# The low parts of four more projection weight blocks are formed on POOL instead of VectorE

## The chip, the cores and the metric

The kernel runs on one core of a Trainium2 chip. The metric is the device time of one execution in microseconds (us); the kernel before took 667.89 us in the median of three runs (666.8 to 670.55).

## The reference, cut to what matters

One layer of a backbone over 512 latent tokens and 256 context tokens of width 1024, float32:

```python
h_lat = modulate(rms_norm(x, norm1_w[layer]), sh1, sc1)
h_ctx = modulate(rms_norm(ctx, norm1_w[layer]), csh1, csc1)
p_lat = h_lat @ w_in[layer]
p_ctx = h_ctx @ w_in[layer]
y_ssd_lat, y_ssd_ctx = ssd_group(...)     # bidirectional Mamba-2 scan
y_ml_lat, y_ml_ctx = mlstm_group(...)     # bidirectional mLSTM
y_lat = concatenate([y_ssd_lat, from_col_major(y_ml_lat, rows)], axis=-1)
x = x + g1 * (y_lat @ w_out[layer])
x = x + g2 * hmoe(modulate(rms_norm(x, norm2_w[layer]), sh2, sc2), ...)
return rms_norm(x, final_norm_w)
```

The columns of `w_in` give z, x, B, C and the step sizes of the Mamba group and the inputs of the mLSTM group. The change lies in the product with `w_in`.

## The kernel before, in words

The product with `w_in` is made in float32r, with three matmuls for one: each operand is split into a high part H, which is the value cast to float32r, and a low part L, which is the value minus H. `mm3` (L255 to L260) adds H times H, H times L and L times H for each of eight slices of 128 rows. Each 256 columns of `w_in` come as two weight blocks of 128 x 1024 (512 KB): block `w3_0` holds slices 0 to 3 of column group 3, `w3_1` slices 4 to 7. A block passes four steps in `unit_w` (L221 to L231): SyncE's queue loads it (`raw_w`, L215, two buffers), ScalarE casts the high part (L224), and then VectorE or POOL subtracts to form the low part. A letter of the string `LENG` (L68), counted over the calls, says which: D is VectorE (L230), P is POOL (L228). High and low parts have three buffers each. The calls run in the order w2 (x), w3 (x), w0 and w1 (z), w4 (B), w5 (C) and on, two letters for each.

```python
        S.copy(wH, raw)
        e_ = LENG[nun[0]]
        nun[0] += 1
        if e_ == "P":
            wsub[0] = G.tensor_tensor(wL, raw, wH, ALU.subtract)
        else:
            V.tensor_sub(wL, raw, wH)
```

The order of the instructions on each engine is not the order of the source. A scheduler sets it when the program is built, by its own cost model; on the chip each engine then runs its list in that order, and semaphores make it wait for its inputs. So a letter of `LENG` can also move other instructions.

Around the change the program does these things side by side:

- `sx_block(1)` multiplies with w3: `sx1_0`, `sx1_1` and `sx1_c` (context). The `z` loop (L622 to L632) multiplies with w0 (`z0`, `z1`) and w1 (`z2`, `z3`). `sx_block(2)` and `sx_block(3)` multiply with w4 (B) and w5 (C). `conv` (L471 to L478) applies a convolution to each result: ScalarE at L473, four VectorE operations at L126, ScalarE's silu.
- `mod_late` (L589 to L606) streams blocks `wl` of 1 MB of the modulation weights (L191, three buffers) and multiplies them at L597 into `modl`; ScalarE copies the sum (`mrl`, L603) and two transposes follow (L606). `wl3_6` is the last block of `mod_late(3)`; `wl4_0` is the first of `mod_late(4)`.
- The gate chain of both groups is on VectorE: a polynomial `gp`, `tsp`, `ga`, then two scans `gF` (L505, L506), which read `ga` and the mask `rmask`, four scans `gm` (L507 to L510), the sums `gG`, `tsp`, `gW` (L520, L521, L118), and `gd`. The mask is three memsets on POOL (L498 to L500); `tsp` is cleared on POOL too (L492). PE's matmul `pgl` (L537) reads `gd`; transposes `gt` (L552, L557) follow, and from them `cw` and `cxw`, which the Mamba stage needs.
- The Mamba stage (L646 to L735) and the mLSTM stage follow, then the experts (MoE) from some 420 us on, where PE multiplies with expert weights that stream in.

Of the kernel before, what the change touches and what calls it, by code (L numbers as in the profile page):

```python
# [64 lines left out]
LASTC = ((0, 512), (512, 256), (768, 256))  # L65
FNS = (1, 3)
RG = [(0, 2), (2, 3), (3, 4)]
LENG = "PPDPDDDPDPDDPPDDDDDDDDPDPPPDPPPP"  # L68
OOB = float(1 << 20)
R2 = 44  # L70
C4N = 9
# [13 lines left out]
def body(tc, a, out, dbg=None):  # L85
# [135 lines left out]
    def unit_w(name, src, sc=None, to=None, raw=None):  # L221
        raw = raw or raw_w(name, src, sc=sc)
        wH, wL = to or (wst.tile([128, 1024], F32R, name=name + q, tag="w" + q, bufs=3)[:, :] for q in "HL")
# [3 lines that stand above are left out]
# [1396 lines left out]
```

## Time and profile before

| | |
|---|---|
| runs | 670.55, 666.8, 667.89 us; median 667.89 |
| profiled execution | 666.7 us, its span 665.0 us |
| PE busy | 606.8 us (91% of the span) |
| VectorE (DVE) busy | 406.8 us (61%) |
| ScalarE (ACT) busy | 271.4 us (41%) |
| POOL busy | 140.8 us (21%) |
| mean granted clock of TensorE | 0.972 of full speed |

PE is the busiest engine, so the places that count are those where PE stands idle or runs at a low clock, and what ends its idle time there. A share of the whole span doesn't tell of them; the table of stretches and the timelines do. The profiled execution lies 1.2 us under the median.

### The profile page before, as it was taken

The page shows a single profiled execution, that of the slowest core. Times are in us where ns is not written, and L with a number is a line of the kernel's source. Part 1 is how long each engine was busy: PE and PEld are TensorE (multiplying, and loading weights), DVE is VectorE, ACT ScalarE, POOL GpSimd, SP SyncE. Part 2 cuts the span into 40 slices and gives each one's busy share as a digit, 9 for nine tenths or more (in the row PEclk, how much of TensorE's full clock was granted, in tenths as well). Part 3 has the DMA queues.
Part 4 walks back from the last instruction along what each step waited for, and adds up shares of the span by engine and source line. Part 5 has one row for each costly group of instructions (what it writes and reads, how often), then busy time and mean ns, then how long its engine had stood idle before and what let it go on. Part 6 is the DMA issues. An engine that isn't in the chain of part 4 may idle for free. (4 is left out here: it accounts for less than half of the span.)

```text
span 665.0 us, 11431 instructions
## 1 busy us (share of the span) xinstructions
PE 606.8 (91%) x4315; PEld 414.7 (62%) x4315; DVE 406.8 (61%) x870; ACT 271.4 (41%) x580; POOL 140.8 (21%) x141
## 2 busy tenths in 40 slices
PE   4898997998899999999998995889999999998992
PEld 3574764787777888999998885524433334433341
DVE  2758996358756656545989765435555555555465
ACT  5435623428625694464254343122222222222325
POOL 2202000203776430023748010000000000000003
PEclk9999997999999999899999999799999999999996
DMA  8885787214435751137033798599999999999913
GB/s 342 313 292 192 299 293 281 91 38 134 162 108 184 283 178 34 31 122 268 14 118 125 289 416 372 209 422 422 426 423 425 391 382 398 410 424 412 411 66 126
DMA packets 35163, 171.64 MB, mean 258 GB/s; under 512 B 4435, under 2 KB 6051, under 8 KB 22052
## 3 DMA queue, kind: packets, MB, share of 16 engines
q1 hardware_dynamic: 31568, 162.68, 63.2%
q0 software_dynamic: 2448, 6.30, 2.4%
q10 hardware_dynamic: 1092, 1.93, 0.8%
q8 instruction: 34, 0.56, 0.3%
q14 instruction: 21, 0.17, 0.1%
HBM read 169.21 MB, written 4.30 MB: 261 GB/s over the span
## 5 line engine op out<-in xcount | busy, mean ns | idle before, releaser
L1308 PE MATMUL gu<-we,xT 128*32 128x512 f32 (+1 forms) x736 | 98.7, 603 | 0.6 <-DVE xT L123 0.6
L118 DVE TENSOR_TENSOR x1t<-x1t,pa 128x512 f32<-128x512 f32 (+1 forms) x108 | 66.2, 663 | 50.2 <-PE pa L1308 50.0
L1308 PEld LDWEIGHTS gu<-we,xT 128*32 128x32 f32 (+1 forms) x736 | 26.1, 114 | 50.3 <-issue 42.7
L1220 POOL DMA_INDIRECT xg<-xnd,tabi x13 | 13.2, 1015 | 192.9 <-PE xt L1308 166.9
L1308 PE MATMUL yy<-we,hTm 128*32 128x512 f32 (+2 forms) x384 | 49.1, 578 | 1.9 <-ACT hTm L1346 1.0
L1336 ACT ACTIVATE hid<-gu 128x256 f32<-128x256 f32 x13 | 5.0, 385 | 107.2 <-PE gu L1308 107.2
L1308 PE MATMUL pa<-yH,oh 128*128 128x512 f32 (+1 forms) x108 | 47.7, 445 | 0.5 <-DVE x1t L118 0.5
L1308 PE MATMUL pa<-yL,oh 128*128 128x512 f32 (+1 forms) x108 | 41.8, 391 | 0.8 <-DVE yL L1362 0.8
L1308 PEld LDWEIGHTS pa<-yH,oh 128*128 128x128 f32 x108 | 20.2, 188 | 31.5 <-issue 12.6
L1321 ACT ACTIVATE xT<-xt,mv,mv 128x128 f32<-128x128 f32 x78 | 29.8, 455 | 19.1 <-DVE xT L123 19.1
L228 POOL TENSOR_TENSOR w_1L<-w,w_1H 128x1024 fp32r<-128x1024 f32 x5 | 12.2, 2437 | 101.1 <-ACT w_1H L224 101.1
L1308 PEld LDWEIGHTS yy<-we,hTm 128*32 128x32 f32 (+1 forms) x384 | 14.8, 113 | 27.9 <-issue 21.6
L126 DVE SCALAR_TENSOR_TENSOR cv<-sx,pc,cv 128x510 f32<-128x510 f32 (+1 forms) x32 | 23.7, 741 | 11.2 <-ACT cv L473 10.9
L118 DVE TENSOR_TENSOR yf<-yy,g2b 128x512 f32<-128x512 f32 (+1 forms) x27 | 18.1, 672 | 18.9 <-PE yy L1308 17.5
L1361 ACT CAST yH<-yf 128x512 fp32r<-128x512 f32 (+1 forms) x27 | 16.2, 601 | 31.1 <-DVE yf L118 31.1
L1362 DVE TENSOR_TENSOR yL<-yf,yH 128x512 fp32r<-128x512 f32 (+1 forms) x27 | 19.0, 704 | 13.0 <-ACT yH L1361 12.2
L1308 PEld LDWEIGHTS pa<-yL,oh 128*128 128x128 f32 x108 | 20.4, 190 | 5.6 <-issue 1.4
L228 POOL TENSOR_TENSOR w_0L<-w,w_0H 128x1024 fp32r<-128x1024 f32 x3 | 7.6, 2547 | 74.7 <-ACT w_0H L224 74.7
L711 ACT ACTIVATE sg<-sg,cu 128x128 f32<-128x128 f32 x64 | 19.6, 388 | 9.4 <-POOL sg L648 9.4
L597 PE MATMUL modl<-wl,cs 128*32 128x256 f32 x256 | 18.1, 382 | 2.7 <-DMA wl<-in_w_mod_dram 2.7
L282 PE MATMUL mod<-wm,cs 128*32 128x256 f32 x128 | 12.2, 443 | 7.9 <-DMA wm<-in_wm_dram 7.9
L1308 PEld LDWEIGHTS xt<-ident,xg 128*128 128x128 f32 x104 | 12.0, 144 | 11.7 <-issue 10.9
(539 smaller groups left out, 1676.0 us busy)
## 6 DMA issues: line engine op xcount, KB each, us to landing
we<-in_wex_dram SPq DMA_DIRECT2D x94, 1024.0 KB, 8.1
wl<-in_w_mod_dram SPq DMA_DIRECT2D x16, 1024.0 KB, 5.7
w<-in_win_dram SPq DMA_DIRECT2D x24, 512.0 KB, 4.1
wm<-in_wm_dram SPq DMA_DIRECT2D x8, 1024.0 KB, 5.4
sg<-rowS SPq DMA_DIRECT2D x8, 512.0 KB
sw<-rowS SPq DMA_DIRECT2D x8, 512.0 KB, 4.9
xin<-in_xr_dram SPq DMA_DIRECT2D x4, 512.0 KB
mg<-rowM SPq DMA_DIRECT2D x4, 512.0 KB
```

Source lines behind the costliest of these rows:

```text
L118: return (eng or V).tensor_tensor(o, x, y, op)
L126: return V.scalar_tensor_tensor(o, x, s, y, o1, o2)
L228: wsub[0] = G.tensor_tensor(wL, raw, wH, ALU.subtract)
L282: T.matmul(pm_[j:j + 32, 0:256], cs[:, q, :], wm[:, q, :], start=(q < 4), stop=(q >= 4))
L597: T.matmul(ps[32 * j:32 * j + 32, 0:256], cs[:, k + q, :], wm[:, q, j], start=(k + q == 0), stop=(k + q == KB - 1))
L711: S.activation(gb[:, h], gb[:, h], AF.Exp, bias=cu[:, c, 12 * d + h:12 * d + h + 1])
L1220: G.indirect_dma_start(out=xg, out_offset=None, in_=xnd, in_offset=bass.IndirectOffsetOnAxis(ap=idx, axis=0), bounds_check=SEQ - 1, oob_is ...
L1308: chain[0] = f(*args, **kw)
L1321: S.activation(xT[:, k], pt[:, q * 128:(q + 1) * 128], AF.Identity, bias=B2[:, k:k + 1], scale=A2[:, k:k + 1])
L1336: silu = S.activation(hid_t, gu[:, 0:256], AF.Silu)
L1361: S.copy(yH, yf)
L1362: V.tensor_sub(yL, yf, yH)
```

## The change

One line:

```diff
-LENG = "PPDPDDDPDPDDPPDDDDDDDDPDPPPDPPPP"
+LENG = "PPDPPPPPPPDDPPDDDDDDDDPDPPPDPPPP"
```

Described as five blocks of x, z and B, it alters four letters: those with index 4, 5, 6 and 8, which are `w0_0`, `w0_1` and `w1_0` (z) and `w4_0` (B). `w3_0` (x, index 2) stays on VectorE. The scheduler then sets other orders on all engines. In the rows below, names carry buffer numbers; `hlH4` and `hlL4` are the high and low part of slice 4 of the latent activations.

POOL, from the last low part of x to the last of B (the difference, with + for the kernel with the change):

```order
 L228 TENSOR_TENSOR w3_1L_772<-w3_1_769,w3_1H_771 128x1024
+L228 TENSOR_TENSOR w0_0L_998<-w0_0_995,w0_0H_997 128x1024
 L492 MEMSET tsp_658 128x768
+L228 TENSOR_TENSOR w0_1L_1004<-w0_1_1001,w0_1H_1003 128x1024
 L498 MEMSET rmask_663 44x768
 L499 MEMSET rmask_663 32x6
 L500 MEMSET rmask_663 12x6
+L228 TENSOR_TENSOR w1_0L_1062<-w1_0_1059,w1_0H_1061 128x1024
 L228 TENSOR_TENSOR w1_1L_1068<-w1_1_1065,w1_1H_1067 128x1024
+L228 TENSOR_TENSOR w4_0L_1223<-w4_0_1220,w4_0H_1222 128x1024
 L228 TENSOR_TENSOR w4_1L_1229<-w4_1_1226,w4_1H_1228 128x1024
```

The three memsets of the mask now stand behind the low part of `w0_1`, which waits for ScalarE's cast of `w0_1`.

PE around `pgl`, the matmul that ends the gate chain, before:

```order
L260 MATMUL z0_1007<-hlH5_463,w0_1H_1003 128x512
L260 MATMUL z0_1007<-hlL5_464,w0_1H_1003 128x512
L260 MATMUL z0_1007<-hlH5_463,w0_1L_1004 128x512
L260 MATMUL z0_1007<-hlH6_509,w0_1H_1003 128x512
L537 MATMUL pgl_699<-gd_696,ones_81 128x288
L552 MATMUL gt5_716<-ident_76,tsp_658 128x128
L260 MATMUL z0_1007<-hlL6_510,w0_1H_1003 128x512
```

and with the change:

```order
L260 MATMUL z2_1071<-hlL3_353,w1_0H_1061 128x512
L260 MATMUL z2_1071<-hlH3_352,w1_0L_1062 128x512
L260 MATMUL z2_1071<-hlH4_409,w1_1H_1067 128x512
L260 MATMUL z2_1071<-hlL4_410,w1_1H_1067 128x512
L537 MATMUL pgl_699<-gd_696,ones_81 128x288
L552 MATMUL gt5_716<-ident_76,tsp_658 128x128
L260 MATMUL z2_1071<-hlH4_409,w1_1L_1068 128x512
```

`pgl` has moved from within `z0` to within `z2`, some thirty matmuls of 128x512 later.

PE in the first half of z, with the change (before, `wl4_0` stood between `z0` and `z1`, and the transposes of `modl3` within `z0`):

```order
L260 MATMUL z0_1007<-hlL3_353,w0_0H_997 128x512
L260 MATMUL z0_1007<-hlH3_352,w0_0L_998 128x512
L597 MATMUL modl3_947<-wl3_6_978,cs_92 32x256 x8
L606 MATMUL modl3_947<-ident_76,mrl3_988 128x128 x2
L260 MATMUL z1_1033<-hlH0_227,w0_0H_997 128x512
L260 MATMUL z1_1033<-hlL0_228,w0_0H_997 128x512
```

The last modulation block now stands directly ahead of the transposes that need ScalarE's copy of its result. On SyncE's queue, the loads of `w1_1`, `w4_0` and `w4_1` have moved ahead of `wl4_6` and `wl5_0` to `wl5_4`.

## Rows read from the trace of the kernel before

**Rows 1.** The profile's part 1: engine, busy us, share, instructions.

```profile
PE 606.8 (91%) x4315; PEld 414.7 (62%) x4315; DVE 406.8 (61%) x870; ACT 271.4 (41%) x580; POOL 140.8 (21%) x141
```

**Rows 2.** Busy time by stretch, columns in the first row (PEclk: granted clock).

```profile
core 0: us, PE busy (x) PEld busy (x) DVE busy (x) ACT busy (x) POOL busy (x), PEclk, DMA share, GB/s
82.40:106.06 23.66, 18.73 (x182) 11.94 (x181) 23.30 (x38) 7.19 (x10) 0.00 (x0) 0.99 0.83 299
106.06:112.50 6.44, 6.44 (x14) 4.14 (x15) 3.27 (x10) 2.93 (x3) 0.00 (x0) 0.50 0.62 190
112.50:129.88 17.38, 17.38 (x93) 12.46 (x92) 5.21 (x21) 6.54 (x10) 4.07 (x2) 1.00 0.37 133
160.00:220.00 60.00, 51.31 (x427) 44.20 (x425) 41.36 (x49) 34.01 (x87) 41.10 (x28) 0.97 0.51 171
425.00:665.00 240.00, 221.38 (x1478) 93.98 (x1470) 127.77 (x234) 65.83 (x162) 17.72 (x18) 0.97 0.90 366
```

**Rows 3.** PE's timeline, 82 to 146: start, duration, instruction, [idle before <-releaser].

```profile
82.50 2.79 PE L597 MATMUL modl<-wl,cs 128*32 128x256 f32 x46
...
88.88 1.02 PE L597 MATMUL modl<-wl,cs 128*32 128x256 f32 x10 [0.40 <-DMA wl<-in_w_mod_dram]
89.83 0.50 PE L260 MATMUL z<-hlH,w_0H 128*128 128x512 f32 x1
...
92.79 1.07 PE L597 MATMUL modl<-wl,cs 128*32 128x256 f32 x16
...
102.72 1.07 PE L597 MATMUL modl<-wl,cs 128*32 128x256 f32 x16 [2.27 <-DMA wl<-in_w_mod_dram]
106.06 0.79 PE L260 MATMUL z<-hlH,w_1L 128*128 128x512 f32 x1 [2.27 <-DVE w_1L L230]
...
108.49 1.33 PE L537 MATMUL pgl<-gd,ones 44*128 44x288 f32 x2
...
145.46 0.39 PE L260 MATMUL sx<-hlH,w_0H 128*128 128x512 f32 x1
```

**Rows 4.** ScalarE's timeline, 82 to 96, same columns.

```profile
85.35 0.37 ACT L603 COPY mrl<-modl 128x256 f32<-128x256 f32 x1 [2.11 <-PE modl L597]
...
92.67 1.05 ACT L224 CAST w_1H<-w 128x1024 fp32r<-128x1024 f32 x1 [4.31 <-PE z L260]
```

**Rows 5.** POOL's timeline, 50 to 160.

```profile
53.59 0.75 POOL L498 MEMSET rmask<- 44x768 f32 x1
...
120.96 2.42 POOL L228 TENSOR_TENSOR w_1L<-w,w_1H 128x1024 fp32r<-128x1024 f32 x1 [66.31 <-ACT w_1H L224]
...
153.19 2.80 POOL L228 TENSOR_TENSOR w_0L<-w,w_0H 128x1024 fp32r<-128x1024 f32 x1 [16.80 <-ACT w_0H L224]
```

**Rows 6.** VectorE's timeline, 66 to 154.

```profile
66.25 1.21 DVE L230 TENSOR_TENSOR w_0L<-w,w_0H 128x1024 fp32r<-128x1024 f32 x1
...
69.19 0.75 DVE L126 SCALAR_TENSOR_TENSOR cv<-sx,pc,cv 128x510 f32<-128x510 f32 x1 [0.47 <-ACT cv L473]
...
92.79 1.74 DVE L505 TENSOR_TENSOR_SCAN gF<-rmask,ga 32x768 f32<-32x768 f32 x1
...
104.79 1.22 DVE L230 TENSOR_TENSOR w_1L<-w,w_1H 128x1024 fp32r<-128x1024 f32 x1
...
106.68 0.51 DVE L118 TENSOR_TENSOR gd<-ident,gl 44x144 f32<-44x144 f32 x2
...
122.08 2.38 DVE L230 TENSOR_TENSOR w_0L<-w,w_0H 128x1024 fp32r<-128x1024 f32 x1 [4.29 <-ACT w_0H L224]
...
146.77 2.03 DVE L126 SCALAR_TENSOR_TENSOR cv<-sx_c,pc,cv 128x254 f32<-128x254 f32 x4
...
153.62 2.04 DVE L126 SCALAR_TENSOR_TENSOR cv<-sx_c,pc,cv 128x254 f32<-128x254 f32 x4
```

**Rows 7.** The DMA queue of SyncE, around 83.6: issue time, time to issue.

```profile
83.61 0.37 SPq L191 DMA_DIRECT2D wl<-in_w_mod_dram  x1
```

## The prediction

> **What bounds the kernel now.** I read part 1 of the profile first: PE is busy for 606.8 of 665.0 us, VectorE for 406.8, POOL for 140.8 [rows 1]. So VectorE as a whole is no bound, and 1.2 us taken from it four times is worth nothing unless PE waits there. The table of stretches says where PE waits [rows 2]. From 82.40 to 106.06 PE is busy for 18.73 us only, and VectorE for 23.30: here VectorE is full and PE loses 4.93 us. From 106.06 to 112.50 PE is busy throughout, at a granted clock of 0.50, the lower of its two levels (1.2 GHz instead of 2.4): half of 6.44, or 3.2 us, is lost. After that it has 1.00 and no idle time until 129.88. The experts' stretch from 425 on is PE's too (221.38 of 240), with the DMA at 0.90; nothing there depends on the four blocks, so I take it that a shift in the early part is passed on whole.
>
> PE's timeline names the losses [rows 3]: 0.40 before 88.88 (a modulation block), 2.27 before 102.72 (another), 2.27 before 106.06 (the low part of `w0_1`, VectorE's, at L230), together 4.94. The clock falls after the last two. With the clock's 3.2 that is **8.1 us between the end of `sx1_c` (82.4, just ahead of the modulation at 82.50 [rows 3]) and the first matmul of C (145.46)**. I balance this stretch before and after: the matmuls in it are the same, so the time changes by idle time and clock alone.
>
> **What comes off VectorE.** Four subtractions of 1.2 us [rows 6] leave it.
> - `w0_0` stood at 66.25, and VectorE's chain restarts at 69.19 behind ScalarE, after idle time: nothing gained.
> - `w0_1` stood at 104.79, in the gate chain between the scans and `gd`: it shortens that chain by 1.2, and it is the wait of 2.27.
> - `w1_0` stood behind `gd`; `w4_0` at 122.08 had waited 4.29 for ScalarE: nothing.
>
> **What POOL gets.** Each subtraction takes it 2.42 [rows 5]. `w0_0` has its cast long before PE needs it: nothing. `w0_1` waits for ScalarE's cast, which waits for the last matmul of `z1` with `w0_0` (it ended 4.31 of idle time on ScalarE, at 92.67 [rows 4]). **Behind it on POOL now stand the memsets of the mask.** Before, they began at 53.59, with 0.75 for the large one [rows 5], long before the first scan at 92.79 [rows 6]. This is the new wait: POOL's cast wait, then VectorE's scans, then `gd`, then PE at `pgl`.
>
> **When PE arrives at `pgl`.** I replay PE's new order with the old durations. `sx1_c` now starts 0.35 earlier (four matmuls of a modulation block went behind it), and ends at 82.05.
> - 19 matmuls of modulation (46 rows took 2.79, two rows for one matmul [rows 3]): 2.3; twelve of `z0`: 2.9, as `z1`'s twelve took from 89.83 to 92.79. It is 87.35 with a tenth or so at each change of shape.
> - `wl3_6`: its buffer comes free at some 82.8, and a block issued at 83.61 was first used at 88.88, 5.27 later [rows 7, 3]. So it lands at 88.07, **0.7 idle**. Its eight matmuls last 0.95, then ScalarE's copy, **0.65 idle** (0.37 for the copy [rows 4] and the way there and back, my estimate), transposes 0.25: 90.1.
> - `z1` with `w0_0`: 2.9, so 93.0. The cast of `w0_1` takes 1.05 [rows 4] and ends at 94.0; PE has some modulation to do, **0.3 idle**. POOL's subtraction 94.05 to 96.47; PE runs dry at 95.3, **1.2 idle**.
> - Then `sx1_c` again, the rest of `z0` and `z1`, `z2` with `w1_0` and two with `w1_1`, all as before: 11.0. **PE is at `pgl` at 107.5**, with 2.85 lost.
>
> **When `gd` is ready.** The mask is done 0.95 after 96.47, so the first scan starts at 97.4 instead of 92.79. From that scan to the end of `gd` (106.68 + 0.51 = 107.19) it was 14.4; less the subtraction of `w0_1` (and 0.1 for another operation that has moved) 13.1 to 13.5: `gd` at 110.9, if nothing else disturbs the chain.
>
> But POOL now subtracts `w1_0` and `w1_1` beside it, 2.42 each. No row shows a scan beside a subtraction of POOL, so I bound it. A VectorE subtraction that began at 122.08, while POOL's ran from 120.96 to 123.38, took 2.38 instead of 1.22 [rows 6, 5]: it stood until POOL was done. The convolution's four operations at 153.62, beside POOL's at 153.19, took 2.04 against 2.03 alone [rows 6, 5]: nothing. These read PSUM and SBUF, the subtraction reads SBUF twice. The scans `gF` read `ga` and `rmask`, both SBUF, and the sums behind them too; they are nearest to the subtraction, so I take nearly the whole of two, 4.6, and keep 0 as the other end. A gain I exclude, because a second user takes no work off the chain. `gd` is at **115.5** (110.9 at the other end), and PE stands at `pgl` for **8.0** (3.4).
>
> The Trainium skill has a rule on this (SBUF — State Buffer, section "Who interferes with whom"): a VectorE instruction with two SBUF inputs shares a read interface with a GpSimd instruction that reads SBUF, one with at most one SBUF input does not. By that rule the stretch comes out about 5 us longer; without it, about 0.6 longer. The subtraction and the convolution in the trace agree with it, and no run here shows a scan under it.
>
> **The sum.** A wait of 2.27 twice put the clock to 0.50 for 6.44 [rows 2, 3], so one longer wait is taken to cost 1.6 to 3.2. Behind `pgl` the order has `wl4_6` later, 0.3. Losses: 2.85 + 8.0 + 1.6 to 3.2 + 0.3 = 12.75 to 14.35. Against 8.1, and with 0.35 of an earlier start: **4.3 to 5.9 later, 5.1 taken**. From 160 to 220 the orders of PE, POOL and SyncE change too; PE has 8.7 of idle time there [rows 2], which I cannot replay: nothing taken, 2 either way kept. So 666.7 + 5.1 = 671.8 for the profiled execution, and as the median lies 1.2 above it, **673.0**; its own range 670 to 676. Without the half percent of 667.89, 3.3 us, no measurement here tells a change from none: faster begins at 664.6, slower at 671.2.
>
> **The rivals.**
> - *The scans run beside POOL undisturbed.* For it: no row shows them together. Against: the subtraction. Then the wait is 3.4 and the losses 8.15 to 9.75; against 8.1, and the 0.35, between 0.3 less and 1.3 more, with the median at about **668.4**. No change.
> - *PE does not stand at `pgl`.* PE has been given some thirty matmuls of z ahead of it, and the two waits of 2.27 and the fall of the clock are gone. It decides from the point at which the scans start by 94 and PE comes to `pgl` after `gd`: the cast and subtraction of `w0_1` would have to come three microseconds earlier, or the mask. Then 3.2 lost against 8.1, and 0.35: 5.3 less, **662.6**. Against it: the cast's wait for `z1` and the memsets' place behind it are in the order.
> - *The clock falls twice.* The small waits between 87 and 97 add up to 2.85 in ten microseconds, and before, two waits of 2.27 were enough. Another 3.2 of clock: **676.2**. Against it: 0.40 before 88.88 was followed by the full clock.
>
> That the change moves other blocks than it names is no rival of its own: the order shows four moved, and the sum is of those.
>
> **How the numbers follow.** Forecast 0.52, no contention 0.22, no wait at `pgl` 0.12, two falls of the clock 0.14. Of the forecast's 0.52 some 0.10 ends under 671.2, as the bounds of the later stretch reach there; of the second case 0.04 ends above, and 0.01 under 664.6; of the third 0.02 stays within. Faster 0.11, same 0.29, slower 0.60. The range goes from 666.8, which holds the second case, to 677.0, which holds most of the last; the third case and the tails are left out.
>
> **What would show it.** Right: `gF` starts at about 97, with VectorE waiting for POOL's memset; PE's longest idle time before 145 ends at `pgl`, by `gd`; scans or sums of 2 us and more beside POOL's subtractions; a granted clock of 0.50 behind `pgl`; the first matmul of C near 150.5. Scans of unchanged length would show the second case, `pgl` without a wait the third. The prediction is wrong if C starts before 148, or if the time between C and the end changes by more than 2.

## The result and the profile after

The changed kernel took **676.12 us** in the median (675.37 to 680.35, six runs), beside 668.11 (663.54 to 671.62, six runs) for the kernel before on the same chips: a ratio of 1.012, with a 95% interval of 1.0086 to 1.0154. It is slower by 8.0 us. The forecast was 673.0, or 5.1 slower, with a range from 666.8 to 677.0 that holds the result. Executions that lie more than 1.5% above the fastest of their kernel are left out of the ratios, here and below, but not out of the medians; without them two rows of the table below would have 669.62 instead of 670.68 and 663.55 instead of 664.84.

The profiled execution has a span of 674.4 us, 9.4 more than before. Part 1 of its profile, as in [rows 1]:

```profile
PE 609.7 (90%) x4315; PEld 415.6 (62%) x4315; DVE 404.1 (60%) x866; ACT 268.1 (40%) x578; POOL 148.1 (22%) x145
```

VectorE has lost 2.7 us and POOL gained 7.3; PE is busy for 2.9 us more. PE's timeline from the end of `sx1_c` on, columns as in [rows 3]:

```profile
87.65 1.07 PE L597 MATMUL modl<-wl,cs 128*32 128x256 f32 x16 [0.62 <-DMA wl<-in_w_mod_dram]
...
89.21 0.44 PE L606 MATMUL modl<-ident,mrl 128*128 128x128 f32 x2 [0.49 <-ACT mrl L603]
...
95.85 0.50 PE L260 MATMUL z<-hlH,w_1L 128*128 128x512 f32 x1 [0.72 <-POOL w_1L L228]
...
114.88 1.29 PE L537 MATMUL pgl<-gd,ones 44*128 44x288 f32 x2 [8.14 <-DVE gd L118]
```

The two waits of 2.27 [rows 3] are gone. In their place are three small ones (0.62, 0.49, 0.72) and one of 8.14 at `pgl`, ended by VectorE's `gd`. POOL's and VectorE's timelines say why it is so late (columns as in [rows 5] and [rows 6]):

```profile
93.39 2.40 POOL L228 TENSOR_TENSOR w_1L<-w,w_1H 128x1024 fp32r<-128x1024 f32 x1 [29.28 <-ACT w_1H L224]
95.74 0.73 POOL L498 MEMSET rmask<- 44x768 f32 x1
...
98.86 3.54 POOL L228 TENSOR_TENSOR w_0L<-w,w_0H 128x1024 fp32r<-128x1024 f32 x1 [2.08 <-DMA w<-in_win_dram]
102.36 2.83 POOL L228 TENSOR_TENSOR w_1L<-w,w_1H 128x1024 fp32r<-128x1024 f32 x1
```

```profile
96.66 1.75 DVE L505 TENSOR_TENSOR_SCAN gF<-rmask,ga 32x768 f32<-32x768 f32 x1 [3.87 <-POOL rmask L499]
98.42 1.75 DVE L506 TENSOR_TENSOR_SCAN gF<-rmask,ga 12x768 f32<-12x768 f32 x1
100.18 2.77 DVE L507 TENSOR_TENSOR_SCAN gm<-ga,gli 32x256 f32<-32x256 f32 x1
102.98 2.75 DVE L508 TENSOR_TENSOR_SCAN gm<-ga,gli 12x256 f32<-12x256 f32 x1
...
114.22 0.52 DVE L118 TENSOR_TENSOR gd<-ident,gl 44x144 f32<-44x144 f32 x2
```

The first scan `gF` waits 3.87 for the mask, which POOL clears behind `w0_1`. Then the two short scans of `gm`, 0.68 each before, take 2.77 and 2.75: POOL's subtractions of `w1_0` and `w1_1`, from 98.86 and 102.36 on, lie beside them, and take 3.54 and 2.83 themselves instead of 2.42. The stretches of PE, columns as in [rows 2]:

```profile
81.71:106.60 24.89, 23.06 (x157) 16.45 (x156) 20.80 (x22) 6.43 (x10) 9.61 (x6) 1.00 0.60 215
106.60:114.88 8.28, 0.14 (x1) 0.03 (x1) 7.84 (x21) 2.65 (x3) 0.00 (x0) 0.64 0.17 60
114.88:119.60 4.72, 4.72 (x13) 2.94 (x13) 1.46 (x9) 0.00 (x0) 0.00 (x0) 0.55 0.03 6
119.60:150.40 30.80, 30.63 (x222) 20.88 (x222) 8.34 (x25) 8.96 (x13) 4.80 (x2) 1.00 0.54 206
```

From the modulation behind `sx1_c` to the first matmul of C it was 62.96 us before (82.50 to 145.46: 58.02 busy, 4.94 idle); now it is 68.69 (81.71 to 150.40: 58.55 busy, 10.14 idle). So this stretch is 5.7 longer, 5.2 of it idle time, and starts 0.8 earlier. The rest of the 9.4, 4.5, comes later. From the first matmul of C to the end:

```profile
145.46:665.00 519.54, 479.30 (x3419) 325.04 (x3417) 312.71 (x685) 209.28 (x485) 123.34 (x107) 0.97 0.67 262
```

```profile
150.40:674.40 524.00, 482.20 (x3419) 327.17 (x3417) 311.39 (x685) 208.90 (x485) 119.74 (x109) 0.97 0.67 261
```

That is 519.54 before and 524.00 now: 1.6 more idle time, and 2.9 more of PE's busy time for the same 3419 rows. The granted clock tells of the 2.9. Two stretches of after, and the same work before:

```profile
280.00:286.20 6.20, 6.20 (x30) 6.20 (x30) 2.96 (x10) 2.54 (x4) 0.00 (x0) 0.50 0.00 0
...
364.80:368.30 3.50, 2.83 (x15) 2.53 (x13) 2.53 (x10) 0.75 (x2) 0.09 (x1) 0.51 0.93 391
```

```profile
276.00:280.00 4.00, 4.00 (x24) 4.00 (x22) 2.71 (x9) 2.49 (x4) 0.00 (x0) 0.57 0.00 0
356.07:358.35 2.28, 1.60 (x15) 1.41 (x14) 2.28 (x11) 0.59 (x1) 1.91 (x2) 1.00 0.00 0
```

In the first PE ran at the lower level for 6.2 us and a little around them, some 7 in all, where before it was 3.4 of 4 us (0.57): 3.6 more, of which half, 1.8, is lost. In the second it was busy for 2.83 us at the lower level, where the same matmuls before took 1.60 at the full clock: 1.2 more. Together these make up the 2.9. Where the 1.6 of idle time come from isn't shown.

### The profile page after: what moved, and what is told of

Read it like the earlier page. It is cut to its first block, busy times and chain, and to the rows that moved or that the text cites. A ratio compares the mean times of both kernels' runs of the same rounds, so it can differ in the third digit from the quotient of the medians.

```text
span 674.4 us, 11434 instructions
## 1 busy us (share of the span) xinstructions
PE 609.7 (90%) x4315; PEld 415.6 (62%) x4315; DVE 404.1 (60%) x866; ACT 268.1 (40%) x578; POOL 148.1 (22%) x145
## 5 line engine op out<-in xcount | busy, mean ns | idle before, releaser
L1220 POOL DMA_INDIRECT xg<-xnd,tabi x13 | 13.2, 1015 | 192.7 <-PE xt L1308 166.4
L228 POOL TENSOR_TENSOR w_0L<-w,w_0H 128x1024 fp32r<-128x1024 f32 x6 | 15.6, 2607 | 97.1 <-ACT w_0H L224 95.1
L228 POOL TENSOR_TENSOR w_1L<-w,w_1H 128x1024 fp32r<-128x1024 f32 x6 | 15.0, 2508 | 59.6 <-ACT w_1H L224 59.6
L711 ACT ACTIVATE sg<-sg,cu 128x128 f32<-128x128 f32 x64 | 19.6, 389 | 13.3 <-POOL sg L648 13.2
L282 PE MATMUL mod<-wm,cs 128*32 128x256 f32 x128 | 12.2, 444 | 7.6 <-DMA wm<-in_wm_dram 7.6
```

Of the source, the lines that this page charges most:

```text
L282: T.matmul(pm_[j:j + 32, 0:256], cs[:, q, :], wm[:, q, :], start=(q < 4), stop=(q >= 4))
L711: S.activation(gb[:, h], gb[:, h], AF.Exp, bias=cu[:, c, 12 * d + h:12 * d + h + 1])
L1220: G.indirect_dma_start(out=xg, out_offset=None, in_=xnd, in_offset=bass.IndirectOffsetOnAxis(ap=idx, axis=0), bounds_check=SEQ - 1, oob_is ...
```

## The experiments

Each was timed beside the kernel before on the same chip, but for the two with added work on POOL, of which there is one profile each. `LENG` of the kernel before ends in the same letters as the change's; only its first 12 are shown. The times, with the profiled executions' events (us from the span's start; "wait" is PE's longest idle time between 81 and 130; "beside" are POOL's subtractions that ran beside the gate chain, from the first scan to `gd`):

| kernel | gF starts | beside | gd ends | wait | C starts | median | ratio, 95% interval |
|---|---|---|---|---|---|---|---|
| before | 92.79 | none | 107.19 | 2.27 | 145.46 | 668.11 | |
| the change | 96.66 | w1_0, w1_1 | 114.74 | 8.14 | 150.40 | 676.12 | 1.012 (1.0086 to 1.0154) |
| again | 96.19 | w1_0, w1_1 | 114.23 | 8.09 | 153.56 | 676.10 | 1.0149 (1.0094 to 1.0204) |
| mask first | 91.75 | w0_1, w1_0, w1_1 | 111.91 | 5.98 | 152.56 | 676.22 | 1.0117 (1.0079 to 1.0154) |
| w0_1 alone | 96.81 | w1_1 | 113.10 | 6.00 | 146.93 | 670.68 | 1.0043 (1.0008 to 1.0078) |
| all but w0_1 | 92.74 | w1_0 | 109.10 | 6.58 | 148.83 | 672.05 | 1.0053 (1.0017 to 1.0089) |
| all but w1_0 | 97.22 | w1_1 | 114.04 | 6.04 | 149.26 | 671.07 | 1.0045 (1.0009 to 1.0081) |
| w0_0, w4_0 | 92.62 | none | 107.02 | 4.35 | 146.18 | 667.71 | 0.9983 (0.9948 to 1.0017) |
| w1 on VectorE | 94.89 | none | 110.30 | 4.00 | 144.35 | 667.73 | 1.0007 (0.9968 to 1.0046) |
| mask first, w1 on VectorE | 92.97 | w0_1 | 109.83 | 2.61 | 145.85 | 666.49 | 0.998 (0.9938 to 1.0023) |
| w0_1 before gm | 90.74 | none | 106.94 | 1.12 | 138.72 | 661.77 | 0.9916 (0.988 to 0.9951) |
| w0_1 before gF | 95.13 | w1_1 | 111.39 | 2.21 | 142.21 | 664.84 | 0.9933 (0.9899 to 0.9968) |

The modulation behind `sx1_c` doesn't begin at the same time in each of them: at 82.50 before, 81.71 with the change, 81.24 in its second profile, 80.85 with the mask first, 82.26 in all but `w1_0`, 79.93 with w1 on VectorE, 80.45 in `w0_1` before `gm`. Where events of two kernels are compared below, it is by their distance from it. And as each `LENG` sets other orders on all engines, two rows of the table never differ by one delay alone.

**The change again**, unaltered.

> The kernel with the change, once more. Theory: the first scan gF starts at 96 to 97 behind the mask's memsets, PE waits 8 us at pgl, the first matmul of C is at 150 to 151, the time 675 to 678. Still open: between the first matmul of C and the end the change took some 4.5 us more than the kernel before. If that comes of the new order, the stretch is again about 524 us; if it comes of falls of the clock that differ between executions, it lies anywhere between 519 and 525.

It took 676.10, and the chain went as before. But C began at 153.56, 3.2 us later and outside what was expected, and from there to the end it took 520.3 us, not 524.0. Ahead of C the granted clock makes the difference; the row of this run, and the same place in the first profile:

```profile
114.37:127.60 13.23, 13.23 (x32) 8.49 (x33) 3.49 (x23) 3.17 (x6) 0.00 (x0) 0.50 0.01 2
```

```profile
114.88:119.10 4.22, 4.22 (x12) 2.70 (x12) 1.20 (x7) 0.00 (x0) 0.00 (x0) 0.50 0.03 7
```

Behind the same wait of 8 us PE ran at the lower level for 13.2 us here, and for 4.2 in the first profile; the stretch behind C had less of it here. So the 4.5 us behind C don't belong to the new order as such: the same program passes there in 0.8 more than the kernel before. Of the 3.7 between its two executions, 1.8 is busy time of PE for the same 3419 rows, which is the clock, and 1.8 is idle time, whose cause isn't shown. Falls of the clock differ in place and length between two executions of one program.

**The mask first.** The four lines stand ahead of the gate polynomial:

```diff
+    rmask = c4("rmask", TOK, parts=R2)
+    G.memset(rmask, 1.0)
+    G.memset(rmask[0:32, 0:TOK:128], 0.0)
+    G.memset(rmask[32:R2, 127:TOK:128], 0.0)
     ge = c4("ge", TOK, parts=R2)
```

> The change, with the mask's memsets written ahead of the gate polynomial, so that they stand ahead of the low part of w0_1 on POOL. Theory: gF starts at 92.7 as before, 4 us earlier than with the change; the subtractions of w0_1, w1_0 and w1_1 on POOL then all meet the scans and cost up to 2.4 each, so gd is ready at 110 to 113 instead of 114.7, PE waits 4 to 6 us at pgl instead of 8.1, and the time is 672 to 674. Rival, that the memsets' place is not what counts: the wait stays at 8, the time at 676.

```profile
91.75 1.74 DVE L505 TENSOR_TENSOR_SCAN gF<-rmask,ga 32x768 f32<-32x768 f32 x1
93.50 3.81 DVE L506 TENSOR_TENSOR_SCAN gF<-rmask,ga 12x768 f32<-12x768 f32 x1
...
98.74 3.47 DVE L509 TENSOR_TENSOR_SCAN gm<-ga,gm,gli 32x512 f32<-32x512 f32 x1
102.24 3.27 DVE L510 TENSOR_TENSOR_SCAN gm<-ga,gm,gli 12x512 f32<-12x512 f32 x1
```

```profile
111.27 0.77 PE L260 MATMUL z<-hlH,w_0H 128*128 128x512 f32 x1 [5.98 <-DVE cv L126]
```

A miss. Counted from the modulation, `gF` starts 4 us earlier, as meant, and now all three subtractions meet scans: 3.81 instead of 1.75, 3.47 and 3.27 instead of 1.27. Of the 4 us `gd` keeps 1.9. PE waits 6 us, now ahead of `z2`, for a convolution (`cv`) that stands on VectorE behind the scans (that it must free `z2`'s accumulator is read from the program, which has three of them), and the time is the same, with 15 us at the lower clock behind the wait (rows at the end of the next section). Putting the mask first doesn't take the cost away.

**w0_1 alone**: `PPDPDPDPDPDD`.

> The kernel before, with w0_1 alone on POOL. Theory: the mask stands behind it, gF starts at 96 to 97; one subtraction of POOL (w1_1) meets the scans instead of two, so gd is ready near 112, PE waits 4 to 6 us at pgl, and the time is 671 to 674. Rival, that the sum of the moved blocks counts and not this one: 668.

670.68 lies just under the range. PE waits for the low part of `w1_0`, on VectorE behind the chain. POOL's `w1_1` began 0.06 us behind the last scan, which kept its 1.27. POOL's instruction took 3.40 instead of 2.42, and then a copy of 32x3 elements behind the scan was held up by it:

```profile
103.05 1.27 DVE L510 TENSOR_TENSOR_SCAN gm<-ga,gm,gli 12x512 f32<-12x512 f32 x1
104.36 2.18 DVE L513 COPY mprev<-gm 32x3 f32<-32x3 f32 x1
```

```profile
103.11 3.40 POOL L228 TENSOR_TENSOR w_1L<-w,w_1H 128x1024 fp32r<-128x1024 f32 x1 [6.18 <-ACT w_1H L224]
```

The same copy took 0.16 before. Here it stood until POOL was done, at 106.51.

**All but w0_1**: `PPDPPDPPPPDD`.

> The change without w0_1, whose low part stays on VectorE. Theory: the mask is early and gF starts at 92.7; the subtractions of w1_0 and w1_1 on POOL may still meet the scans gm, 2 to 4.6 us; pgl again stands within z0, so PE waits 2 to 5 us in all ahead of it; the time is 668 to 671. Rival, that late scans are the whole cost and POOL beside them none: 666 to 668.

```profile
98.98 3.24 DVE L510 TENSOR_TENSOR_SCAN gm<-ga,gm,gli 12x512 f32<-12x512 f32 x1
```

672.05 is a little above the range. With the mask early, the last scan of `gm` took 3.24 instead of 1.27 beside `w1_0`, and PE waits 6.58 for the low part of `w0_1`. The measure for this is not the 2.27 of before, where a block of modulation split the wait in two, but the 4.35 of the next run, in which PE has no such block there and the scans are undisturbed: 2.2 more. The rival, that POOL beside the scans is no cost, is out.

**w0_0 and w4_0 alone**: `PPDPPDDPPPDD`.

> The kernel before, with only w0_0 and w4_0 on POOL, the two blocks whose subtraction the prediction put at nothing. Theory: neither runs beside the scans and the mask stays ahead of them; gF starts at 92 to 93, all six scans keep their length, the first matmul of C is at 145 to 147, the time 667 to 670. Rival, that any block moved to POOL costs some 2 us, whichever it is: 671 to 673.

667.71, no change: the two blocks that don't meet the chain cost and bring nothing that these runs can tell.

**POOL beside the scans, by itself.** Two kernels with the `LENG` of before and added work on POOL ahead of the scans:

```diff
+    gW = c4("gW", TOK, parts=R2)
+    for _ in range(2):
+        tt(gW, ga, gli, ALU.subtract, G)
```

```diff
+    gW = c4("gW", TOK, parts=R2)
+    G.tensor_copy(gW[:, 0:1], ga[:, 0:1])
+    for _ in range(3):
+        G.memset(gW, 0.0)
```

> The kernel before, with two added subtractions of 44x768 on POOL that read ga and gli and so start with the scans; their result isn't used. By the time of a 128x1024 subtraction (2.42) each takes some 1.8. Theory: scans and subtractions hold each other up, so the six scans together take up to 3.6 more than the 7.39 of before. Rival, no contention: 7.4 in sum, each scan as before.

> The kernel before, with three added memsets of 44x768 on POOL (0.75 each), which start with the scans and read nothing. Theory, that it is POOL's reading that holds a scan up: the six scans take 7.4 us in sum as before. Rival, that any work of POOL's beside a scan holds it up: 9 to 9.7.

Subtractions, VectorE and POOL:

```profile
95.06 3.38 DVE L508 TENSOR_TENSOR_SCAN gF<-rmask,ga 32x768 f32<-32x768 f32 x1
```

```profile
94.33 2.50 POOL L118 TENSOR_TENSOR gW<-ga,gli 44x768 f32<-44x768 f32 x1
```

Memsets:

```profile
92.59 1.74 DVE L509 TENSOR_TENSOR_SCAN gF<-rmask,ga 32x768 f32<-32x768 f32 x1
94.34 1.75 DVE L510 TENSOR_TENSOR_SCAN gF<-rmask,ga 12x768 f32<-12x768 f32 x1
```

```profile
92.65 2.32 POOL L508 MEMSET gW<- 44x768 f32 x3
```

Only the second subtraction fell beside a scan, and that scan took 3.38 instead of 1.74: it stood until POOL's instruction ended at 96.83. The six scans took 9.03 in sum, within what was expected, instead of 7.39. Three memsets beside the same scans changed nothing: 7.39. So a POOL instruction that reads holds a scan up, and one that only writes doesn't. The times of these two, 668.54 and 670.78, are of one execution each, and nothing is read from them. The rule of the Trainium skill that the prediction weighed (SBUF — State Buffer, "Who interferes with whom") says this of VectorE's instructions with two SBUF inputs without naming scans; these runs show it for scans. The section also counts copies among those that can take the shared ports, which agrees with the copy of 2.18 above.

**Both halves of w1 on VectorE**: `PPDPPPDDPPDD`, and the same with **the mask first**.

> The change with both halves of w1 on VectorE; the mask stays behind w0_1. Theory: gF starts at 96 to 97 and the scans keep their length (7.4 in sum), since no subtraction of POOL meets them; gd is ready near 110 to 112, with one or two subtractions of 1.2 in the chain; PE waits 3 to 5 us, 668 to 672. Rival, that the late mask alone makes the cost: PE waits 8 and the time is 675 to 677.

> The change with the mask's memsets ahead of w0_1 and both halves of w1 on VectorE. Only the subtraction of w0_1 (2.4) is left beside the scans. Theory: gF starts at 92, the scans take 7.4 + up to 2.4, gd is ready at 107 to 109, if w1's subtractions stand behind it; PE waits 2 to 4 us ahead of pgl or behind; the time is 667 to 671. Rival, that the new order on PE and not the scans costs the time: 674 to 677.

667.73 and 666.49: neither can be told from the kernel before. In the first the mask is still 4 us late:

```profile
94.89 1.75 DVE L505 TENSOR_TENSOR_SCAN gF<-rmask,ga 32x768 f32<-32x768 f32 x1 [3.88 <-POOL rmask L499]
...
98.41 0.68 DVE L507 TENSOR_TENSOR_SCAN gm<-ga,gli 32x256 f32<-32x256 f32 x1
```

```profile
107.65 0.51 PE L260 MATMUL z<-hlH,w_0L 128*128 128x512 f32 x1 [4.00 <-DVE w_0L L230]
```

`gF` waits 3.88 for POOL as in the change, but the scans keep their length, PE's longest wait is 4.00, and the 8 us are gone. In the second only `w0_1` meets a scan (3.81 instead of 1.75), and PE waits 2.61. Both came out just under what was expected.

**All but w1_0**: `PPDPPPDPPPDD`.

> The change without w1_0, whose low part stays on VectorE; the mask stays behind w0_1, and of POOL's subtractions only w1_1, as in the kernel before, can meet the chain. Theory, that two subtractions of POOL beside the chain are what costs: one of them is left, 669 to 672, between the run with both halves of w1 on VectorE (667.7) and the change (676.1). Rival, that w1_0 alone is it: 667 to 669; rival, that the late mask is it: 675 to 677.

```profile
102.17 3.28 DVE L509 TENSOR_TENSOR_SCAN gm<-ga,gm,gli 32x512 f32<-32x512 f32 x1
```

```profile
101.46 2.91 POOL L228 TENSOR_TENSOR w_1L<-w,w_1H 128x1024 fp32r<-128x1024 f32 x1 [4.12 <-ACT w_1H L224]
```

671.07, as expected. With the mask late in all three, no subtraction beside the chain takes 667.7, one (`w1_1`) 671.1, two (the change) 676.1; from the modulation to C it is 64.4, 67.0 and, in the two profiles of the change, 68.7 and 72.3. The intervals of none and one overlap, that of two stands clear of both.

**VectorE forms w0_1 early.** `LENG` of before; the code from the scans of `gm` (in the second kernel from those of `gF`) to `cxw` is written behind the splitting of w0:

```diff
...
+    us0 = [quad(unit_w(f"w0_{i}", a["win"][i])) for i in range(2)]
     scan(gm[f, SEQ:TOK], ga[f, SEQ:TOK], gli[f, SEQ:TOK], NEG, ALU.add, ALU.max)
...
     sz = c8z("sz", 4, 512)
     for blk in range(2):
-        wH, wL = load_w(blk)
+        wH, wL = load_w(blk, us0 if blk == 0 else None)
```

> The kernel before, its LENG too, with the scans gm and what follows up to cxw written behind the loading and splitting of w0, so that VectorE forms w0_1's low part between the scans gF and gm instead of behind gW. Theory: PE has w0_1 some 7 us earlier, works on z0, z1 and part of z2 while the chain runs, comes to pgl at some 107 with gd ready at 107 to 109; the losses of 8.1 fall to 2 to 5; 663 to 666. Rival, that the wait only moves to pgl or to w1_0's low part: 668.

> As the run before, but with gF's scans moved as well, so that w0_1's low part stands ahead of all scans. Theory: w0_1 is ready at 95, gF starts at 95, gd is ready at 108 to 110, 1 to 2 us later than before; PE waits 1 to 3 us; 663 to 667. Rival, that the later chain costs PE what it gains: 668 to 670.

```profile
92.51 1.75 DVE L506 TENSOR_TENSOR_SCAN gF<-rmask,ga 12x768 f32<-12x768 f32 x1
94.37 1.22 DVE L230 TENSOR_TENSOR w_1L<-w,w_1H 128x1024 fp32r<-128x1024 f32 x1
95.50 0.67 DVE L565 TENSOR_TENSOR_SCAN gm<-ga,gli 32x256 f32<-32x256 f32 x1
```

```profile
106.20 0.51 PE L260 MATMUL z<-hlH,w_0L 128*128 128x512 f32 x1 [1.12 <-DVE w_0L L230]
...
108.02 0.75 PE L595 MATMUL pgl<-gd,ones 44*128 44x288 f32 x2
```

```profile
80.45:138.72 58.27, 56.04 (x383) 39.56 (x383) 39.69 (x78) 17.81 (x25) 4.99 (x4) 1.00 0.57 201
```

The first is the fastest kernel here: **661.77 us**, faster than the kernel before by 0.5 to 1.2%. `w0_1`'s subtraction takes 1.22 between the scans. `gd` is ready 26.5 us behind the start of the modulation, 1.8 later than before, but PE has enough of z to do until then: its longest wait is 1.12, and from the modulation to the first matmul of C it takes 58.27 us, all at the full clock, for 62.96 before. The time is under the range expected. With `w0_1` ahead of `gF` too, the chain is later (`gd` at 111.39, not 108 to 110) and POOL's `w1_1` falls beside it; 664.84, as expected.

## Why the prediction came out so

- **Where PE waits, and why: right.** PE's wait at `pgl` was forecast at 8.0 and is 8.14; the scans' start at 97.4 (96.66), `gd` at 115.5 (114.74), the first matmul of C at 150.5 (150.40).
- **POOL beside the scans: right.** Forecast at 4.6 more; the six scans took 11.56 instead of 7.39, 4.2 more. The added subtractions and memsets show the mechanism by itself, so the rival of undisturbed scans is out.
- **The mask as the new wait: there, and no cost by itself.** The first scan does wait for it, 3.87. The prediction's own sum has it so: with the mask late and the scans undisturbed it came to a wait of 3.4 at `pgl` and 668.4. The run with w1 on VectorE is this case: a mask 3.88 late, scans of the old length, a longest wait of 4.00, and 667.73. What the step did not see is that an early mask doesn't help either: then `w0_1` meets a scan too, and the time is the same 676. What turns the late chain into a cost is POOL's subtractions of w1.
- **Nothing from `w0_0` and `w4_0`: right**, 667.71 for these two alone.
- **The terms that were mis-sized are those of the clock and of the stretch behind C.** The clock behind `pgl` was "taken to cost 1.6 to 3.2", and behind C there was "nothing taken, 2 either way kept". In the first profile PE ran at the lower level for 4.2 us behind the wait (2.1 us lost, in the range), and the time behind C grew by 4.5. In the second it ran so for 13.2 (6.6 lost, twice the upper end), and behind C it was 0.8. So the profiled executions came out 9.4 and 8.9 behind that of before, and the medians 8.0, where 5.1 was forecast.
- **By its own sign the prediction fails in the first profile**: it was to be wrong "if the time between C and the end changes by more than 2", and that changed by 4.5. The second profile, with 0.8, shows that this time is no fixed effect of the change. The other kernels of the table have 518.4 to 524.7 there, and the two highest (w1 on VectorE, and `w0_1` before `gF`) are not slower in the median than the kernel before.
- **The sum ahead of C came out with some luck.** The small waits were forecast at 2.85 and are 1.83, so idle time and clock add up to 12.2, under the 12.75 to 14.35. The 0.35 of "an earlier start" should not have been taken off: the four matmuls that moved behind `sx1_c` are still done ahead of C, and the stretch has 393 rows instead of 385. The rest of PE's added busy time there, about 1 us by an estimate (58.55 less 2.1, against 58.02 less 3.2, less 0.5 for the four matmuls), isn't explained by any run. These errors nearly cancel in the 150.5.
- **The clock falls twice: the number, not the cause.** This rival's 676.2 is what was measured. But its second fall was to come of the small waits between 87 and 97, and from 81.71 to 106.60 PE had the full clock (1.00). The result lies at the upper edge of the forecast's own range (670 to 676), and the wider range holds it because this rival was put in.
- **No wait at `pgl`** did not come about by this change. The kernel with `w0_1` before `gm` shows that the 5 us which that rival priced are to be had, by another way: a short wait, no fall of the clock ahead of C, 5.9 us less in the median (661.77 against 667.70 beside it). In its profile the stretch from the modulation to C is 4.7 shorter; that the modulation begins 2.05 earlier there, and that the time behind C is 2.1 longer, is not explained by any run.

What stays open is what sets the length of a fall of the clock: a wait of 5.98 (the mask first) was followed by at least 15.2 us at the lower level, one of 6.00 (w0_1 alone) by some 3, and no run here took the wait away while it left the rest as it was. What the idle time behind C comes from, 1.6 more in the first profile, stays open too.

The rows for this last point:

```profile
111.27:126.50 15.23, 15.23 (x36) 9.33 (x36) 4.10 (x26) 5.67 (x7) 0.00 (x0) 0.50 0.09 33
```

```profile
111.59:114.50 2.91, 2.91 (x7) 1.89 (x7) 1.86 (x7) 0.00 (x0) 0.00 (x0) 0.50 0.47 149
...
115.00:115.50 0.50, 0.50 (x3) 0.33 (x3) 0.22 (x1) 0.00 (x0) 0.00 (x0) 1.00 0.77 188
```

## What to carry to other kernels

Work that goes from VectorE to POOL can cost more than it frees where VectorE is running a chain that somebody waits for: look up what VectorE does in the very microseconds in which POOL will read, and count each overlapping instruction with up to the other's whole length. Look at the clock behind a new wait as a cost of its own, and one that a single profile doesn't fix: here 2.1 and 6.6 us behind the same wait of 8.1. And when an operand stands behind a long chain on a full engine, try to put it into the chain earlier before giving it to another engine: here the kernel with a subtraction of 1.2 us put ahead of four scans is 6 us faster.

## What the runs showed of the hardware that was not expected

A copy of 32x3 elements (0.16 us alone) took 2.18 beside a subtraction on POOL: the smallest instruction of a chain can wait for nearly the whole of the other's. POOL is held up as well: its subtraction of 2.42 took 3.54 between scans. And the same program, after the same wait of 8.1 us at the same place, had the lower clock for 4.2 us of work in one execution and for 13.2 in another, and the two took 676.08 and 675.56 us.
